# A transformer block on one core: the order of its first step, and where 128 side pieces are worked off

## The chip, the cores and the metric

The kernel runs on one core of a Trainium2 chip. The metric is the device time of one execution in microseconds (us), less is better. The kernel before takes 1694.38 us, the median of three runs between 1694.19 and 1694.40 us. The engines are named as in the profile: PE does the matrix products, DVE the work on vectors, ACT activations and copies, POOL small odd jobs and some transfers, SP issues most transfers.

## The reference

One layer works on 256 latent tokens and 256 context tokens of 2048 channels. Cut to what matters here:

```
h   = rms_norm(x) * g1 * (1 + scale) + shift          # shift, scale from silu(cond) @ w_ada + b_ada
p   = h @ w_in                                        # keys and values of all tokens, queries and gates of the latent ones
a   = grouped-query attention;  b = differential attention    # 2-D rotary, one softmax over latent and context keys
m   = sigmoid(g_a) * (a @ w_br_a) + sigmoid(g_b) * (b @ w_br_b)
x2  = x + gate * (m @ w_out)                          # gate: another chunk of w_ada
out = x2 + gate2 * swiglu_ffn(modulated rms_norm(x2)) # shift, scale, gate2: the last chunks of w_ada
```

Context tokens have a shift and a scale of their own. All of it is in 32-bit floats. The conditioning product `silu(cond) @ w_ada` has six chunks of 2048 columns.

## The kernel before, in words

**Products in three parts.** Every large product is made of three matmuls (`mm3`, L241 to L243): the weight is divided into a high part `whi` and a remainder `wlo`, the activation likewise. A weight tile of 128 x 1024 comes by a transfer of 512 KB into `wraw` (7 buffers, shared with the conditioning pieces `wada`), ACT casts it to `whi` (L235, 3 buffers) and DVE subtracts to get `wlo` (L237, 3 buffers). One such load feeds 24 matmuls of 512 columns. The second matmul of each three, L242, is the one that needs `wlo`.

**The start.** Conditioning vectors come in a small tile `head`, are turned on PE into `hps` (L108) and copied to `cst` and `vt` (L109, L111). The chunks shift and scale of the first norm are made on PE from pieces of `w_ada` (L315, tile `ada`), copied out by ACT (`asb`), turned on PE (`atp`, L325), summed by DVE (L328), and the bias is added (L331), then 1 + scale times g1 (L335). The function `ada_cond` does this in the steps of `STEPS`: one k-tile of 128 channels, one more, then 2, 4, 4 and 4. Meanwhile the second half of the tokens (the latent ones, tiles 2 and 3) and the context tokens (0 and 1) are squared, normed and, for the first k-tile, turned on PE (`xtp`, L378); ACT and DVE make the modulated high and low parts (L391 to L393). `keep_busy` issues idle 128 x 128 transposes on PE (L371). `kv_first` makes the key and value products of the first k-tile (L402).

**Channel steps.** Steps 1 to 5 go over the remaining channels. In each, `kv_group` runs the six column groups of keys and values, for four token tiles at once, and adds the sums from the PSUM tiles `mm` into the tiles kb, ka, vb, va (L443, DVE). In steps 3 to 5 a column group has two weight loads. During the last two groups of a step, DVE makes the modulated tiles of the next one (`hx` L357, `xT` and `cT` L361, eight of each).

**The pieces.** Four more chunks of `w_ada` are computed on DVE: `ada_later` is a generator of 128 pieces (L460 and L458), each with a transfer of 512 KB and one DVE instruction on 128 x 1024 elements. `take(later, n)` lets n pieces go at a place in the program. When a chunk is complete, `ada_row` sums it over partitions with four matmuls (`adac`), adds a row that POOL loads (`adac_sb`, and `adac_g` for one chunk, both from a pool `scr` of 3 buffers), and writes it to DRAM.

**After the steps.** Attention follows with the query and gate projections in between. A gate tile takes a buffer of the same pool `scr` when ACT evacuates it (L859), and POOL sends it to DRAM (`gate_d`, L860). Then come the merge (the product with `w_bra`, then `w_out`), and the feed-forward part.

**What sets the order.** A framework orders each engine's instructions before the run, from the program's order, its own estimates and `issue_after`. On the chip every engine takes its instructions strictly in that order, and waits for semaphores at the head. SP's and POOL's transfers are queues of the same kind.

Of the kernel before, what the change touches and what calls it, by code (L numbers as in the profile page):

```python
# [46 lines left out]
def hybrid_block(ctx: ExitStack, tc: tile.TileContext, t: dict, out: bass.AP):  # L47
# [35 lines left out]

    cst = scratch("cst", CG, tag="sq", bufs=2).rearrange("p (k m) -> p k m", m=32)
# [7 lines left out]
    ssq, r_tok = sums[:, 0:16].rearrange("p (i q) -> p i q", i=4), sums[:, 20:24]  # L92
    nc.gpsimd.memset(sums, EPS)
# [4 lines left out]
    def load_tokens(src, i):  # L98

        tok_in[i] = big_tile(f"tok{i}")  # L100
        for h in range(2):
            nc.sync.dma_start(out=tok_in[i][:, h * 2 * CG:(h + 1) * 2 * CG],
                              in_=src[0, i % 2 * P:(i % 2 + 1) * P, h * 2 * CG:(h + 1) * 2 * CG])
# [4 lines left out]
    nc.tensor.transpose(out=hps[:, 0:81], in_=head, identity=ident[0:81, 0:81])  # L108
# [6 lines left out]
    gsub = vt[:, 80:81]  # L115

# [10 lines left out]
    def squares_act(i, c0=CG, c1=3 * CG, late=None, to=0):  # L127
        mid = tok_in[i][:, c0:c1]
        with tc.issue_after(late.ins) if late else nullcontext():
            nc.scalar.activation(out=mid, in_=mid, func=AF.Square, scale=D ** -0.5, accum_out=ssq[:, i, to:to + 1])  # L130

    def squares_dve(i, parts=(0, 3), late=None):
        with tc.issue_after(late.ins) if late else nullcontext():
            for n, q in enumerate(parts):
# [3 lines left out]
                                                      accum_out=ssq[:, i, 1 + n:2 + n])  # L138
# [88 lines left out]
    def split_w(raw, nk, in_big=False, late=None):  # L227
# [6 lines left out]
        with tc.issue_after(late[0].ins) if late else nullcontext():  # L234
            last_hi.append(nc.scalar.copy(out=hi[:, 0:nk], in_=raw[:, 0:nk]))  # L235
        with tc.issue_after(late[1].ins) if late else nullcontext():
# [43 lines left out]
    def ada_cond(k0, nk):  # L280
# [4 lines left out]
        for part in range(2):  # L285
            aps = s_ps("ada")
            held = []
            for q in range(0, NKT, kk):
# [22 lines left out]
                first_ks, last_ks = (range(0, 4), range(12, 16)) if k0 == 0 else (range(4, 8), range(8, 12)) if k0 == 4 else (range(12, 16), range(0, 4))  # L311
                for k, rhs in held[::-1] if k0 else held:
# [4 lines left out]
                held = []  # L317
                if last:
# [3 lines left out]
                if last:  # L322
                    atp = tp_ps("atp")
                    for j in range(nk):
                        nc.tensor.transpose(out=atp[:, j * P:(j + 1) * P], in_=asb[:, j * P:(j + 1) * P], identity=ident)  # L325
                    m = small(f"mod{part}", 8)
                    mv = m[:, 0:2 * nk].rearrange("p (j w) -> p j w", w=2)
                    nc.vector.tensor_reduce(  # L328
                        out=mv, in_=atp[:, 0:ncol].rearrange("p (j g m) -> p j m g", g=4, m=32)[:, :, 0:2, :],
# [290 lines left out]
    def next_tokens(tok):  # L620
# [7 lines left out]
        if tok == 3:  # L628
            hold(0, (first_hi[-1], last_first[-1]))
# [553 lines left out]
```

## Time and profile before

| | |
|---|---|
| median of three runs | 1694.38 us |
| the profiled execution | 1696.49 us |
| its span | 1694.7 us |
| PE busy | 1675.7 us, 99% of the span |
| DVE busy | 1143.0 us, 67% |
| ACT busy | 776.4 us, 46% |
| transfers | 413.08 MB, mean 244 GB/s |
| an `ada` piece on DVE (L460) | 120 times, mean 1278 ns |
| a `wlo` subtraction on DVE (L237) | 498 times, mean 1220 ns |

About 1.8 us of the profiled execution lie outside its span. A row of the timeline gives the start in us from the span's beginning, the duration, the engine, line, operation, the tile written and those read, and in brackets the idle time before it with what ended it. Durations overlap: the next matmul of 512 columns starts 0.227 us after the one before, though the row says 0.39 us; the next `ada` piece or `wlo` on DVE starts 1.19 or 1.14 us later, a copy of 128 x 512 (L443) 0.60 us and a 128 x 256 instruction (L357, L361) 0.40 us later.

### The profile page before, as it was taken

What the parts mean: (1) busy time and instruction counts of PE and PEld (TensorE: products, weight loads), DVE (VectorE), ACT (ScalarE), POOL (GpSimd) and SP (SyncE); (2) the same over time, 40 slices, a digit from 0 to 9 for tenths busy, and PEclk for the clock granted to TensorE, in tenths of its full rate; (3) what the DMA queues carried; (4) which work ended last, traced back from release to release, by engine and by line L of the source; (5) the groups of instructions that cost most, each with busy time, mean ns of one, the idle gap of its engine ahead of it and who ended that gap; (6) DMA issues with size and microseconds to landing.
All of it is one profiled execution on the core that took longest, in us unless ns stands there. A gap on an engine that the chain in (4) does not pass through costs nothing.

```text
span 1694.7 us, 21499 instructions
## 1 busy us (share of the span) xinstructions
PE 1675.7 (99%) x7889; PEld 1354.8 (80%) x7889; DVE 1143.0 (67%) x1454; ACT 776.4 (46%) x1055; POOL 202.3 (12%) x296
## 2 busy tenths in 40 slices
PE   7999999999999999999999999999999999999998
PEld 5677778887887778888888888888888888888887
DVE  5765779697798888986666755566666666544454
ACT  5231222246666566667544534444444444333332
POOL 0200002011131110011111101111111111100000
PEclk9999999999999999999999999999999999999999
DMA  9888875777767767766877857888888898866662
GB/s 349 300 311 286 299 256 169 237 249 257 231 198 228 247 208 256 265 228 201 266 257 248 293 171 215 250 258 263 266 265 268 263 277 253 240 216 197 214 208 88
DMA packets 181284, 413.08 MB, mean 244 GB/s; under 512 B 15001, under 2 KB 16234, under 8 KB 180922
## 3 DMA queue, kind: packets, MB, share of 16 engines
q1 hardware_dynamic: 168906, 374.17, 67.3%
q0 software_dynamic: 12272, 37.53, 7.4%
q8 instruction: 62, 1.02, 0.3%
q14 instruction: 44, 0.36, 0.1%
HBM read 395.35 MB, written 16.29 MB: 243 GB/s over the span
## 4 chain that ended last, share of the span: by engine, by line
PE 92%; DVE 3%; DMA 2%; ACT 1%; issue 1%; POOL 0%; SPq 0%; DVEq 0%; ACTq 0%; POOLq 0%
PE mm L242 28%; PE mm L241 28%; PE mm L243 28%; PE ada L315 2%; PE ptp L815 1%; DVE wlo L237 1%; PE s L791 1%; PE mm L402 1%; PE o L836 1%; DMA wada<-in_ada_t_dram 1%; DMA wraw<-in_w_ff_gate_dram 0%; ACT whi L235 0%; DMA gate_d<-gate 0%; DMA wraw<-in_w_in_dram 0%; DVE ada L460 0%
## 5 line engine op out<-in xcount | busy, mean ns | idle before, releaser
L237 DVE TENSOR_TENSOR wlo<-wraw,whi 128x1024 fp32r<-128x1024 f32 x498 | 607.0, 1220 | 425.1 <-ACT whi L235 423.8
L235 ACT CAST whi<-wraw 128x1024 fp32r<-128x1024 f32 x498 | 522.8, 1051 | 727.1 <-PE mm L243 624.0
L242 PE MATMUL mm<-wlo,hT 128*128 128x512 f32 x684 | 266.2, 389 | 0.4 <-DVE wlo L237 0.4
L243 PE MATMUL mm<-whi,hT 128*128 128x512 f32 x684 | 266.1, 389 | 0.0
L241 PE MATMUL mm<-whi,hT 128*128 128x512 f32 x684 | 266.1, 389 | 0.0
L241 PE MATMUL mm<-whi,xT 128*128 128x512 f32 x630 | 251.9, 402 | 0.0
L242 PE MATMUL mm<-wlo,xT 128*128 128x512 f32 x630 | 247.3, 393 | 2.7 <-DVE wlo L237 2.7
L243 PE MATMUL mm<-whi,xT 128*128 128x512 f32 x630 | 246.8, 392 | 0.0
L460 DVE SCALAR_TENSOR_TENSOR ada<-wada,vt,ada 128x1024 f32<-128x1024 f32 x120 | 152.1, 1278 | 0.0
L242 PEld LDWEIGHTS mm<-wlo,hT 128*128 128x128 f32 x684 | 128.4, 188 | 27.7 <-DVE wlo L237 0.9
L241 PEld LDWEIGHTS mm<-whi,hT 128*128 128x128 f32 x684 | 128.4, 188 | 26.8
L243 PEld LDWEIGHTS mm<-whi,hT 128*128 128x128 f32 x684 | 128.4, 188 | 26.4
L241 PEld LDWEIGHTS mm<-whi,xT 128*128 128x128 f32 x630 | 118.2, 188 | 33.0 <-issue 6.6
L242 PEld LDWEIGHTS mm<-wlo,xT 128*128 128x128 f32 x630 | 118.8, 189 | 27.6 <-DVE wlo L237 5.0
L243 PEld LDWEIGHTS mm<-whi,xT 128*128 128x128 f32 x630 | 118.5, 188 | 25.8 <-DVE xT L361 0.3
L241 PE MATMUL mm<-whi,fT 128*128 128x512 f32 x354 | 137.5, 388 | 0.5 <-DVE y L1128 0.5
L242 PE MATMUL mm<-wlo,fT 128*128 128x512 f32 x354 | 137.3, 388 | 0.0
L243 PE MATMUL mm<-whi,fT 128*128 128x512 f32 x354 | 137.3, 388 | 0.0
L241 PEld LDWEIGHTS mm<-whi,fT 128*128 128x128 f32 x354 | 66.4, 188 | 15.0 <-issue 0.8
L243 PEld LDWEIGHTS mm<-whi,fT 128*128 128x128 f32 x354 | 66.4, 188 | 13.8
L242 PEld LDWEIGHTS mm<-wlo,fT 128*128 128x128 f32 x354 | 66.4, 188 | 13.7
L241 PE MATMUL mm<-whi,oT 128*128 128x512 f32 x192 | 75.9, 396 | 0.0
(236 smaller groups left out, 2142.7 us busy)
## 6 DMA issues: line engine op xcount, KB each, us to landing
wraw<-in_w_in_dram SPq DMA_DIRECT2D x159, 512.0 KB, 4.9
wada<-in_w_ada_dram SPq DMA_DIRECT2D x128, 512.0 KB, 4.7
wraw<-in_w_ff_gate_dram SPq DMA_DIRECT2D x88, 512.0 KB, 4.6
wraw<-in_w_ff_up_dram SPq DMA_DIRECT2D x88, 512.0 KB, 5.2
wraw<-in_w_ff_down_dram SPq DMA_DIRECT2D x88, 512.0 KB, 4.7
wada<-in_ada_t_dram SPq DMA_DIRECT2D x56, 512.0 KB, 6.6
wraw<-in_w_br_a_dram SPq DMA_DIRECT2D x32, 512.0 KB, 5.0
wraw<-in_w_out_dram SPq DMA_DIRECT2D x32, 512.0 KB, 5.1
```

The source lines that it names most:

```text
L235: last_hi.append(nc.scalar.copy(out=hi[:, 0:nk], in_=raw[:, 0:nk]))
L237: last_lo.append(nc.vector.tensor_tensor(out=lo[:, 0:nk], in0=raw[:, 0:nk], in1=hi[:, 0:nk].bitcast(F32), op=ALU.subtract))
L241: nc.tensor.matmul(ps, lhsT=ah, rhs=wh, start=first, stop=False, skip_group_check=skip)
L242: nc.tensor.matmul(ps, lhsT=ah, rhs=wl, start=False, stop=False, skip_group_check=skip)
L243: return nc.tensor.matmul(ps, lhsT=al, rhs=wh, start=False, stop=last, skip_group_check=skip)
L315: last_pe[0] = nc.tensor.matmul(aps[32 * g:32 * g + 32, 0:ncol], lhsT=cst[:, k, :], rhs=rhs, start=k in first_ks, stop=k in last_ks)
L402: last_pe[0] = nc.tensor.matmul(ps[cg], lhsT=x, rhs=ws0[cg][y], start=(n == 0), stop=(n == 2))
L460: nc.vector.scalar_tensor_tensor(out=dst, in0=wt, scalar=sc[:, 0, kt:kt + 1], in1=dst, op0=ALU.mult, op1=ALU.add)
L791: nc.tensor.matmul(sps[i], lhsT=qT[rows, x, hh, tk * P:(tk + 1) * P], rhs=kT["b", grp][y][rows, hh, :], start=(n == 0), stop=(n == 2))
L815: nc.tensor.transpose(out=tp[:, kt * P:(kt + 1) * P], in_=p[:, kt * P:(kt + 1) * P], identity=ident)
L836: nc.tensor.matmul(op[:, 0:BV], lhsT=pT[:, kt, :], rhs=vb[:, kt, hh * BV:(hh + 1) * BV], start=(kt == 0), stop=(kt == 3))
```

## The change

It has these parts.

- **Start.** Five idle transposes go to PE ahead of `hps`, thirty after it, three after the conditioning pieces of step 0 but the last, and ten before the second token tile (before: six, six and four). For step 0 the transpose of `asb` and the sum on DVE become one product with a selection matrix `sel` (two columns). 1 + scale times g1 is folded into the bias once (`vt_done`), so that L335 goes; wider steps have a multiplication with g1 more.
- **Second latent tile.** Token tile 3 is loaded as a half and two quarters, ahead of the second weight load; its squares are shared by ACT and DVE in quarters. The first weight cast is done in two halves. The products of tile 2 with the second weight stand behind the norm of tile 3.
- **Order of held pieces.** In steps 0, 2 and 3 of `STEPS` (k0 of 0, 2 and 4) the conditioning matmuls go over the held pieces forward instead of backward.
- **Pacing of the side pieces.** In step 3 one per half group, two in the last two groups (before: none, then two); in step 4 one, and two from the third group on (before: one throughout); in step 5 one per group (before: two). Later one at every third turn throughout (before: every second until the keys are done). The rest go in the `w_bra` products and in `w_out`, whose third column group now holds the `drain` and the loading of the row `b_all`, which stood before `w_out`.

```diff
-    nc.tensor.transpose(out=hps[:, 0:81], in_=head, identity=ident[0:81, 0:81])
+    idle = mm_ps("idle")
+    for _ in range(5):
+        nc.tensor.transpose(out=idle[:, 0:P], in_=ident, identity=ident)
+    last_pe = [None]
+    last_pe[0] = nc.tensor.transpose(out=hps[:, 0:81], in_=head, identity=ident[0:81, 0:81])
...
-                first_ks, last_ks = (range(0, 4), range(12, 16)) if k0 == 0 else (range(4, 8), range(8, 12)) if k0 == 4 else (range(12, 16), range(0, 4))
-                for k, rhs in held[::-1] if k0 else held:
+                first_ks, last_ks = (range(0, 4), range(12, 16)) if k0 in (0, 2, 4) else (range(12, 16), range(0, 4))
+                for k, rhs in held if k0 in (0, 2, 4) else held[::-1]:
...
+                if k0 == 0 and not (part and last):
+                    keep_busy(3)
...
+                    if k0 == 0:
+                        nc.tensor.matmul(atp[:, 0:2], lhsT=asb[:, 0:P], rhs=sel, start=True, stop=True)
...
-        nc.vector.scalar_tensor_tensor(out=scale, in0=scale, scalar=1.0,
-                                       in1=g1[:, k0:k0 + nk].unsqueeze(2).to_broadcast([P, nk, 2]), op0=ALU.add, op1=ALU.mult)
...
+    keep_busy(30)
     squares_act(2)
-    squares_dve(2)
+    squares_dve(2, late=vt_done)
...
-    keep_busy(6)
-    drain(ada_cond(*steps[0]))
+    ada_0 = ada_cond(*steps[0])
+    take(ada_0, 2)
+    with tc.issue_after(last_pe[0].ins):
+        turn_first(2)
+    drain(ada_0)
...
-    raws = {cg: load_raw(0, cg * CG) for cg in (2, 4)}
-    load_tokens(t["x"], 3)
+    raws = {2: load_raw(0, 2 * CG)}
+    load_tokens(t["x"], 3, (0, 2, 3, 4))
+    raws[4] = load_raw(0, 4 * CG)
...
     next_tokens(3)
+    hold(4, (last_copy[0], last_first[-1]))
+    kv_first(2, (4, 5), (0, 1))
     kv_first(3, (2, 3))
+    kv_first(2, (4, 5), (2,))
     kv_first(3, (4, 5))
...
-                if si == 3 and n >= 4:
-                    take(later, 2)
-                elif si > 3:
+                if si in (3, 4):
+                    take(later, 2 if n >= (4 if si == 3 else 2) else 1)
+                elif si == 5 and half == 0:
                     take(later, 1)
...
-            take(later, 1 if turns[0] % (3 if a_done else 2) else 0)
+            take(later, 1 if turns[0] % 3 == 0 else 0)
...
-    drain(later)
-    b_all = ada_everywhere("b_all", 2)
...
     for cg in range(4):
-        drain(project(w_out, mT, NKT, cg * CG, out_evac(cg), **(dict(tail=TURN2, hook=tail_hook, in_big=(6, 7)) if cg == 3 else {})))
+        if cg == 2:
+            drain(later)
+            b_all = ada_everywhere("b_all", 2)
+        for k, _ in enumerate(project(w_out, mT, NKT, cg * CG, out_evac(cg), **(dict(tail=TURN2, hook=tail_hook, in_big=(6, 7)) if cg == 3 else {}))):
+            if k in (2, 5, 6) and (cg or k > 4):
+                take(later, 1)
```

**First place: step 4 begins.** DVE, before. The weight of the first group of step 4 is `wraw_1648`; its products go to the PSUM tiles `mm_1644` to `mm_1647`. The tiles `mm_1504` to `mm_1507` belong to the last group of step 3.

```order
L331 TENSOR_TENSOR mod1_1484<-mod1_1484,vt_99 128x8
L237 TENSOR_TENSOR wlo_1651<-wraw_1648,whi_1650 128x1024
L335 SCALAR_TENSOR_TENSOR mod1_1484<-mod1_1484,vt_99 128x8
L206 TENSOR_REDUCE lam_1603<-used_691 128x2
L357 SCALAR_TENSOR_TENSOR hx_1489<-tok_t2_1040,mod1_1484,r_all_447 128x256 x2
L357 SCALAR_TENSOR_TENSOR hx_1497<-tok_t2_1040,mod1_1484,r_all_447 128x256 x2
L357 SCALAR_TENSOR_TENSOR hx_1584<-tok_t2_1040,mod1_1484,r_all_447 128x256 x2
L361 SCALAR_TENSOR_TENSOR xT2_1490<-hx_1489,mod0_1256,xT2_1490 128x256 x2
L361 SCALAR_TENSOR_TENSOR xT2_1490<-hx_1497,mod0_1256,xT2_1490 128x256 x2
L443 TENSOR_TENSOR va0_102<-mm_1504,va0_102 128x512
L361 SCALAR_TENSOR_TENSOR cT_1488<-hx_1584,mod0_1256,cT_1488 128x256
L443 TENSOR_TENSOR va0_102<-mm_1505,va0_102 128x512
```

The same of the change (L237 is now L247, L443 is L472, L357 and L361 are L379 and L383). The weight of that group is `wraw_1723`, the last group of step 3 is in `mm_1579` to `mm_1582`.

```order
L383 SCALAR_TENSOR_TENSOR xT2_1565<-hx_1572,mod0_1314,xT2_1565 128x256
L383 SCALAR_TENSOR_TENSOR cT_1563<-hx_1659,mod0_1314,cT_1563 128x256
L472 TENSOR_TENSOR va0_112<-mm_1580,va0_112 128x512
L379 SCALAR_TENSOR_TENSOR hx_1659<-tok_t2_1091,mod1_1554,r_all_499 128x256
L379 SCALAR_TENSOR_TENSOR hx_1666<-tok_t2_1091,mod1_1554,r_all_499 128x256
L472 TENSOR_TENSOR va0_112<-mm_1581,va0_112 128x512
L383 SCALAR_TENSOR_TENSOR cT_1563<-hx_1659,mod0_1314,cT_1563 128x256
L472 TENSOR_TENSOR va0_112<-mm_1582,va0_112 128x512
L383 SCALAR_TENSOR_TENSOR cT_1563<-hx_1666,mod0_1314,cT_1563 128x256
L379 SCALAR_TENSOR_TENSOR hx_1666<-tok_t2_1091,mod1_1554,r_all_499 128x256
L214 TENSOR_REDUCE lam_1678<-used_742 128x2
L247 TENSOR_TENSOR wlo_1726<-wraw_1723,whi_1725 128x1024
```

The first `wlo` of step 4 stood ahead of the modulated tiles and of all four va sums; it now stands behind the fourth. PE at the same place, of the change:

```order
L253 MATMUL mm_1582<-whi_1621,cT_1023 128x512
L251 MATMUL mm_1719<-whi_1725,xT2_1565 128x512
L251 MATMUL mm_1720<-whi_1725,xT2_1565 128x512
L251 MATMUL mm_1721<-whi_1725,cT_1563 128x512
L251 MATMUL mm_1722<-whi_1725,cT_1563 128x512
L252 MATMUL mm_1719<-wlo_1726,xT2_1565 128x512
```

Four matmuls of the high part now stand ahead of the first with `wlo`; before there was one.

**Second place: step 5 begins.** DVE, before; the weight is `wraw_2215`, and `mm_2123` is the first sum of the last group of step 4.

```order
L328 TENSOR_REDUCE mod1_2103<-atp_2098 128x8
L331 TENSOR_TENSOR mod1_2103<-mod1_2103,vt_99 128x8
L237 TENSOR_TENSOR wlo_2218<-wraw_2215,whi_2217 128x1024
L335 SCALAR_TENSOR_TENSOR mod1_2103<-mod1_2103,vt_99 128x8
L460 SCALAR_TENSOR_TENSOR ada2_1433<-wada2_2195,vt_99,ada2_1433 128x1024
L357 SCALAR_TENSOR_TENSOR hx_2108<-tok_t3_1598,mod1_2103,r_all_447 128x256 x2
```

The change; the weight is `wraw_2324`, and `mm_2218` to `mm_2221` are the last group of step 4.

```order
L472 TENSOR_TENSOR va0_112<-mm_2218,va0_112 128x512
L472 TENSOR_TENSOR va0_112<-mm_2219,va0_112 128x512
L379 SCALAR_TENSOR_TENSOR hx_2306<-tok_t3_1673,mod1_2193,r_all_499 128x256
L472 TENSOR_TENSOR va0_112<-mm_2220,va0_112 128x512
L383 SCALAR_TENSOR_TENSOR cT_2202<-hx_2306,mod0_1939,cT_2202 128x256
L472 TENSOR_TENSOR va0_112<-mm_2221,va0_112 128x512
L379 SCALAR_TENSOR_TENSOR hx_2306<-tok_t3_1673,mod1_2193,r_all_499 128x256
L379 SCALAR_TENSOR_TENSOR hx_2313<-tok_t3_1673,mod1_2193,r_all_499 128x256 x2
L383 SCALAR_TENSOR_TENSOR cT_2202<-hx_2306,mod0_1939,cT_2202 128x256
L383 SCALAR_TENSOR_TENSOR cT_2202<-hx_2313,mod0_1939,cT_2202 128x256 x2
L247 TENSOR_TENSOR wlo_2327<-wraw_2324,whi_2326 128x1024
```

Again the first `wlo` of the step has moved from ahead of the modulated tiles to behind the fourth va sum, here with six small instructions between.

**Third place: the gates in attention.** POOL, before: a pair of gate tiles, with the two row loads for a chunk's sum around its second.

```order
L860 DMA gate_d_2733<-gate_4772 128x512
L467 DMA adac_sb_5188<-in_rows_dram 128x512
L860 DMA gate_d_2733<-gate_4775 128x512
L467 DMA adac_g_5267<-in_rows_dram 128x512
L124 TENSOR_TENSOR rstdo_4815<-rstdo_4815,neghalf_80 128x1
```

The change:

```order
L895 DMA gate_d_2822<-gate_4829 128x512
L496 DMA adac_sb_5372<-in_rows_dram 128x512
L895 DMA gate_d_2822<-gate_4832 128x512
L132 TENSOR_TENSOR rstdo_4872<-rstdo_4872,neghalf_80 128x1
```

The load of `adac_g` is no longer there; it now follows the next pair of gate tiles.

More of the change, by code (lines that the diff above doesn't have):

```diff
@@ L82, in hybrid_block @@
     nc.gpsimd.memset(ones, 1.0)
+    sel = tab.tile([P, 2], F32, name="sel")
+    nc.vector.tensor_reduce(out=sel, in_=ident.rearrange("p (g m) -> p m g", m=32)[:, 0:2, :], axis=AX.X, op=ALU.add)
     cst = scratch("cst", CG, tag="sq", bufs=2).rearrange("p (k m) -> p k m", m=32)
@@ L322, in ada_cond @@
                 if last:
-                    atp = tp_ps("atp")
-                    for j in range(nk):
-                        nc.tensor.transpose(out=atp[:, j * P:(j + 1) * P], in_=asb[:, j * P:(j + 1) * P], identity=ident)
                     m = small(f"mod{part}", 8)
                     mv = m[:, 0:2 * nk].rearrange("p (j w) -> p j w", w=2)
-                    nc.vector.tensor_reduce(
-                        out=mv, in_=atp[:, 0:ncol].rearrange("p (j g m) -> p j m g", g=4, m=32)[:, :, 0:2, :],
-                        axis=AX.X, op=ALU.add)
@@ L331, in ada_cond @@
[L331 to L332 removed]
+                    atp = tp_ps("atp")
+                    base = bada[:, part * NKT + k0:part * NKT + k0 + nk].unsqueeze(2).to_broadcast([P, nk, 2])
+                    gain = g1[:, k0:k0 + nk].unsqueeze(2).to_broadcast([P, nk, 2])
+                    if k0 == 0:
+                        nc.tensor.matmul(atp[:, 0:2], lhsT=asb[:, 0:P], rhs=sel, start=True, stop=True)
+                        ms = atp[:, 0:2].rearrange("p (j w) -> p j w", w=2)
+                    else:
+                        for j in range(nk):
+                            nc.tensor.transpose(out=atp[:, j * P:(j + 1) * P], in_=asb[:, j * P:(j + 1) * P], identity=ident)
+                        nc.vector.tensor_reduce(
+                            out=mv, in_=atp[:, 0:ncol].rearrange("p (j g m) -> p j m g", g=4, m=32)[:, :, 0:2, :],
+                            axis=AX.X, op=ALU.add)
+                        ms = mv
@@ L627, in next_tokens @@
         mod_first(tok)
-        if tok == 3:
-            hold(0, (first_hi[-1], last_first[-1]))
     next_tokens(3)
+    hold(4, (last_copy[0], last_first[-1]))
+    kv_first(2, (4, 5), (0, 1))
     kv_first(3, (2, 3))
+    kv_first(2, (4, 5), (2,))
     kv_first(3, (4, 5))
+    hold(0, (first_hi[-1], last_lo[-1]))
+    ada_1 = ada_cond(*steps[1])
     kv_first(2, (0,))
     next_tokens(0)
-    kv_first(3, (0,), True)
+    kv_first(3, (0,), behind=True)
     kv_first(0, (2, 3))
@@ L640, in hybrid_block @@
     next_tokens(1)
-    kv_first(0, (0,), True)
+    kv_first(0, (0,), behind=True)
     kv_first(1, (2, 3))
```

63 lines of the change are left out of this document (37 added, 26 removed).

## The prediction

> **What bounds the kernel now.** I read the page first, then the list of what PE waited for, whole and by stretches, then PE and DVE row by row where the change works.
>
> ```profile
> PE 1675.7 (99%) x7889; PEld 1354.8 (80%) x7889; DVE 1143.0 (67%) x1454; ACT 776.4 (46%) x1055; POOL 202.3 (12%) x296
> PE 92%; DVE 3%; DMA 2%; ACT 1%; issue 1%; POOL 0%; SPq 0%; DVEq 0%; ACTq 0%; POOLq 0%
> ```
>
> PE is busy for 1675.7 of 1694.7 us, and 92% of the chain that ended last is PE's. The change leaves the large products alone. So it can save only out of the 19 us in which PE stands still, and whatever new wait it gives PE is paid in full. Where are those 19 us? PE's waits over the span (us in total, times, longest):
>
> ```profile
> PE ada L315 <- DMA wada<-in_ada_t_dram: 6.0, 2, 5.3
> PE mm L242 <- DVE wlo L237: 3.1, 4, 1.9
> ```
>
> Busy time by stretches says which stage is loose:
>
> ```profile
> 0.00:17.00 17.00, 7.89 (x81) 5.37 (x81) 3.32 (x14) 4.85 (x10) 2.03 (x12) 1.00 0.88 312
> 17.00:40.00 23.00, 22.03 (x148) 16.03 (x149) 16.26 (x35) 16.69 (x31) 1.66 (x3) 1.00 1.01 389
> 100.00:310.00 210.00, 210.00 (x1003) 164.47 (x1002) 157.26 (x231) 55.34 (x74) 10.59 (x5) 1.00 0.74 259
> ```
>
> After the times come PE, PEld, DVE, ACT and POOL busy, the granted clock (1.00 throughout), the share of the transfers and GB/s. Half the idle time lies in the first 17 us. In the channel steps from 100 to 310 us PE has none at all, while DVE is busy for 157 of 210 us: a stage where an addition to DVE finds no PE time to win, and can only lose some.
>
> **The change part by part.**
>
> Start. PE and the short chain to the first key product:
>
> ```profile
> 2.91 0.37 PE L108 MATMUL hps<-ident,head 81*128 81x81 f32 x1 [2.91 <-ACT head L106]
> 8.54 1.82 PE L315 MATMUL ada<-wada,cst 128*32 128x128 f32 x18 [5.26 <-DMA wada<-in_ada_t_dram]
> 10.77 1.49 PE L371 MATMUL idle<-ident 128*128 128x128 f32 x6
> 12.19 1.51 PE L315 MATMUL ada<-wada,cst 128*32 128x128 f32 x24
> 14.04 1.19 PE L315 MATMUL ada<-wada,cst 128*32 128x128 f32 x22
> 15.29 0.27 ACT L320 COPY asb<-ada 128x128 f32<-128x128 f32 x1 [1.71 <-PE ada L315]
> 15.98 0.17 DVE L328 TENSOR_REDUCE mod<-atp 128x2 f32<-128x8 f32 x1 [1.47 <-PE atp L325]
> 16.18 0.16 DVE L331 TENSOR_TENSOR mod<-mod,vt 128x2 f32<-128x2 f32 x1
> 16.38 0.16 DVE L335 SCALAR_TENSOR_TENSOR mod<-mod,vt 128x2 f32<-128x2 f32 x1
> 17.09 1.19 PE L402 MATMUL mm<-whi,xT 128*128 128x512 f32 x4 [0.92 <-ACT xT L391]
> ```
>
> The conditioning matmuls cost 1.82/18 = 0.10 us at first and 1.19/22 = 0.054 us from 14.04 on: PE runs at half pace until about 4 us after it has become nearly continuously busy, though the granted clock reads 1.00. If the idle transposes bring that on early, a piece of 16 matmuls costs 0.9 instead of 1.6 us. Of the 64 matmuls 42 ran slowly, so 42 x 0.046 = 1.9 us go, and two of the three small DVE steps, 0.4 us: 2.3 us earlier at 17.09. The added transposes stand in the 5.26 us between `hps` and the first piece, so at fast pace they cost nothing; uncovered, thirty cost 30 x 0.11 = 3.3 us. What is late next is the first context tile:
>
> ```profile
> 24.19 0.16 DVE L143 TENSOR_REDUCE sums<-sums 128x1 f32<-128x4 f32 x1 [0.18 <-ACT tok L130]
> 25.01 0.29 DVE L146 TENSOR_SCALAR tok<-tok,sums 128x128 f32<-128x128 f32 x1 [0.66 <-POOL sums L144]
> 25.75 0.38 PE L378 MATMUL xtp<-ident,tok 128*128 128x128 f32 x2
> ```
>
> Its norm comes through DVE, which in the new order first does two subtractions of 1.14 us and two quarters of squares. PE's products of the latent tiles finish 2 us earlier, this chain does not follow all the way. The bounds are 0 and 2.3 us; I take **-0.8**, nearer the lower, since what stands ahead on DVE is about as much as before.
>
> [...]
>
> Forward order of the held pieces. One wait goes:
>
> ```profile
> 62.45 1.06 PE L315 MATMUL ada<-wada,cst 128*32 128x512 f32 x8 [0.72 <-DMA wada<-in_ada_t_dram]
> ```
>
> Backward, the eight begin with the piece that landed last; forward, six that are there go first, 6 x 1.06/8 = 0.8 us, which covers it: **-0.8**, between 0 and that.
>
> Channel steps. Pieces in step 3 go from 8 to 16, in step 4 from 12 to 20, in step 5 from 12 to 6. DVE has room on the average. Its order is what costs. Where step 4 begins, before:
>
> ```profile
> 169.94 1.22 DVE L237 TENSOR_TENSOR wlo<-wraw,whi 128x1024 fp32r<-128x1024 f32 x1
> 179.08 0.39 PE L241 MATMUL mm<-whi,xT 128*128 128x512 f32 x1
> 179.31 0.39 PE L242 MATMUL mm<-wlo,xT 128*128 128x512 f32 x1
> 179.42 0.68 DVE L443 TENSOR_TENSOR va<-mm,va 128x512 f32<-128x512 f32 x1
> ```
>
> This `wlo` was ready at 171.16, 8 us ahead. With the added pieces it now stands behind the fourth va sum, which waits for PE to end the group, at 179.42. Behind that sum (0.60) come two 128 x 256 instructions (0.40 each), one `lam` sum (0.19), then `wlo` itself (1.22): ready at 182.23. PE has four high-part matmuls ahead, so it wants it at 179.08 + 4 x 0.227 = 179.99: **+2.2**. All further products and the DVE work of the group queue behind.
>
> In the middle of step 4 the `wlo` of the third group's second load moves from ahead of a modulation sum to behind it:
>
> ```profile
> 210.08 0.60 PE L325 MATMUL atp<-ident,asb 128*128 128x128 f32 x4
> 210.43 0.47 PE L241 MATMUL mm<-whi,xT 128*128 128x512 f32 x1
> 212.91 0.18 DVE L328 TENSOR_REDUCE mod<-atp 128x8 f32<-128x32 f32 x1
> 213.12 0.17 DVE L331 TENSOR_TENSOR mod<-mod,vt 128x8 f32<-128x8 f32 x1
> ```
>
> The sum cannot start before the transposes end at 210.68. With 0.07 for the signal, 0.21 and 0.09 for the two rows and 1.22 for `wlo` it is ready at 212.27; PE wants it at 210.43 + 0.91 = 211.34: **+0.9**.
>
> Where step 5 begins, the same as at step 4:
>
> ```profile
> 242.82 1.23 DVE L237 TENSOR_TENSOR wlo<-wraw,whi 128x1024 fp32r<-128x1024 f32 x1
> 252.65 0.39 PE L243 MATMUL mm<-whi,cT 128*128 128x512 f32 x1
> 252.88 0.39 PE L241 MATMUL mm<-whi,xT 128*128 128x512 f32 x1
> 254.10 0.68 DVE L443 TENSOR_TENSOR va<-mm,va 128x512 f32<-128x512 f32 x1
> ```
>
> The group ends at 253.04, the fourth va sum starts at about 253.15 and takes 0.60; three hx and three cT follow (6 x 0.40), then `wlo` 1.22: ready at 257.37. Wanted at 252.88 + 0.91 = 253.79: **+3.6**. Two more places are within 0.2 us of waiting; with them the channel steps give **+6.9**. The lower bound is 0, if the engine's order let these through; I see no way past a semaphore at the head of DVE, and take the sum. The upper is 8.5, if also the transfers, now 3 x 512 KB per load in part, land late.
>
> Attention. Two waits for `wlo` between 300 and 800 us, then POOL and PE at their cause, then one piece of the chain of waits:
>
> ```profile
> PE mm L242 <- DVE wlo L237: 2.4, 2, 1.9
> ```
>
> ```profile
> 531.28 0.55 POOL L467 DMA_DIRECT2D adac_sb<-in_rows_dram  x1
> 536.53 0.55 POOL L467 DMA_DIRECT2D adac_g<-in_rows_dram  x1 [4.17 <-issue]
> 628.05 0.50 PE L242 MATMUL mm<-wlo,xT 128*128 128x512 f32 x1 [1.86 <-DVE wlo L237]
> ```
>
> ```profile
> 586.77 6.75 DMA gate_d<-gate
> ```
>
> From 531 on the two rows hold two of three buffers, so the next pair of gates must share one: the chain shows 6.75 us for the transfer of the first, ACT's casts get late, DVE bunches, and at 628.05 PE waits. In the change `adac_g` comes after that pair, and fewer pieces stand on DVE: -2.4. Against it a piece and two subtractions now stand ahead of one `wlo`:
>
> ```profile
> 370.86 1.22 DVE L237 TENSOR_TENSOR wlo<-wraw,whi 128x1024 fp32r<-128x1024 f32 x1
> 372.91 0.40 PE L242 MATMUL mm<-wlo,xT 128*128 128x512 f32 x1
> ```
>
> Added are 1.19 + 2 x 0.33 = 1.85 us against 372.91 - 372.08 = 0.83 us to spare: +1.0. Together **-1.4**, between -2.4 and +1.0.
>
> Merge. Sixteen more pieces, 19 us of DVE and 16 transfers, in a stretch of 170 us where DVE was busy 110: hidden by PE on the average, up to 1 us where they stand ahead of a `wlo`: **+0.3**.
>
> Sum: -0.8 - 0.8 + 6.9 - 1.4 + 0.3 = **+4.2** without what overlaps; the 0.9 at 210 shrinks when PE is already 2 us behind and DVE has caught up, so I take **+3.8**. The profiled execution, 1694.7 us of span and 1.8 around it, would go from 1696.5 to 1700.3; the median stands 2.1 us lower, so **1698.2**.
>
> **The rivals.**
>
> *DVE's order costs nowhere.* Then the 6.9 go, and so do the 1.0 at 371 us and the 0.3 of the merge, which I priced in the same way: -0.8 - 0.8 - 2.4 = -4.0, or 1690.4. For it: DVE is only 75% busy in the channel steps. Against it: the fourth va sum needs PE's last matmul of the group. It decides if the first `wlo` of steps 4 and 5 ends within 0.9 us of the group's end.
>
> *The transposes warm nothing.* Thirty at 1.49/6 = 0.25 us end near 3.3 + 7.4 = 10.7, past the 8.54 of the first piece. Pieces then start 2 us late, reach the fast pace only some 4 us on, and the first product comes 0.8 us later than now instead of earlier: 1.6 us on top, 1699.8. [...]
>
> *The merge chokes.* The second half of each `w_bra` product has four pieces more, 4.8 us of DVE in 10.9. If each of the four runs past the spare there by 0.7 us, 2.8 on top: 1701.
>
> *The gains come whole.* The new waits stand, but the start gives its 2.3 (1.5 more) and attention its 2.4 (1.0 more): 1695.7, no change. For it: 1.5 us of the start are held back only by a chain on DVE that the new order rearranges.
>
> **How the numbers follow.** A measurement here tells 0.2%, 3.4 us, from no change: 1691.0 and 1697.8. My forecast, 1698.2, has 0.49, of which 0.21 lies below 1697.8. The first rival has 0.25, as faster; the second 0.11 and the third 0.07, slower; the fourth 0.08, same. Faster 0.25, same 0.29, slower 0.28 + 0.18 = 0.46. The forecast's own range is 1695.5 to 1700.5. The range over all reaches to the first rival and to the third: 1690.2 to 1701.
>
> **What would show it.** In the changed profile PE should wait for `wlo` some 2 us at about 179 and 3.5 us at about 252, and these two should be the longest in the list after the start. The conditioning matmuls at 8.5 us should cost 0.054 us each, the first key product should start near 15 and the first context product near 25.9. The waits at 62 and 628 should be gone. No wait for `wlo` between 150 and 300 us makes the prediction wrong, whatever the time.

## The result, and the profile after

The change makes the kernel slower: 1706.61 us (median of 6 runs, 1704.26 to 1708.59) against 1694.39 us (6 runs, 1693.48 to 1695.41). The ratio is 1.0070, with a 95% interval of 1.0057 to 1.0083. That is 12 us more where 3.8 were forecast, and outside the range. The profiled execution took 1707.28 us, 10.8 us more than that of before.

The page of the changed kernel:

```profile
span 1705.5 us, 21596 instructions
PE 1686.3 (99%) x7935; PEld 1361.3 (80%) x7935; DVE 1145.5 (67%) x1454; ACT 777.8 (46%) x1056; POOL 194.2 (11%) x297
```

PE stands still for 19.2 us, as before (19.0), yet it is busy for 10.6 us more. With both traces cut at the same matmuls, 4.5 us of this lie in the first 37 us, where idle transposes were added, 2.3 in the stretch up to 103 us and 7.5 in the channel steps up to 317 us; attention is 5.1 us less busy. What it waited for, over the span:

```profile
PE mm L252 <- DVE wlo L247: 5.1, 4, 3.0
PE mm L251 <- ACT whi L245: 2.1, 2, 1.1
PE o L871 <- DVE qT L257: 1.2, 1, 1.2
PE ada L325 <- DMA wada<-in_ada_t_dram: 0.8, 1, 0.8
```

The wait for the first conditioning piece has shrunk from 5.3 us to 0.8. In its place stand waits for weights in the channel steps; the stretch from 100 to 310 us shows them (after the times PE, PEld, DVE, ACT and POOL busy, granted clock, share of the transfers, GB/s):

```profile
100.00:310.00 210.00, 202.03 (x943) 153.73 (x942) 158.17 (x230) 52.74 (x71) 9.07 (x6) 0.98 0.76 273
```

From 100 to 310 us PE was busy all the time before; now it lacks 8 us there, and has done 943 of 1003 instructions. DVE's time over the whole stretch is the same (158.17 against 157.26), so it is its order and the places of its work that have changed. The granted clock is 0.98 there, where it was 1.00.

Where the time went can be read by laying the two traces side by side: the start of the same matmul with `wlo` in both (worked out from the two traces: after less before, at the times of before):

```
before, us   37.8  102.7 176.6 192.9 213.5 233.6 250.4 266.7 301.5 555.6 578.6 620.5 646.6 812.6 1687.5
difference  -0.97  +0.34 +0.54 +5.12 +7.06 +9.46 +10.2 +15.5 +15.8 +14.8 +12.8 +15.2 +11.4 +9.57 +10.29
```

Four stairs of the channel steps make it, and attention gives some back. A chunk's row sum on PE (`adac`), 1.2 us, has moved between stretches; it is taken out where sums are named below. One correction to the description ahead: of the 128 pieces 96 come from `ada_later`; the other 32 are those of the feed-forward's modulation.

PE where step 4 begins, after the change:

```profile
179.62 0.61 PE L251 MATMUL mm<-whi,xT 128*128 128x512 f32 x2
181.27 0.49 PE L251 MATMUL mm<-whi,cT 128*128 128x512 f32 x1 [0.43 <-DVE va L472]
183.38 0.75 PE L252 MATMUL mm<-wlo,xT 128*128 128x512 f32 x1 [1.62 <-DVE wlo L247]
183.93 0.63 PE L253 MATMUL mm<-whi,xT 128*128 128x512 f32 x1
184.36 0.63 PE L251 MATMUL mm<-whi,xT 128*128 128x512 f32 x1
186.49 0.57 PE L251 MATMUL mm<-whi,xT 128*128 128x512 f32 x1
186.90 0.40 PE L252 MATMUL mm<-wlo,xT 128*128 128x512 f32 x1
```

DVE ahead of it, and its busy time in the stretch that leads there:

```profile
180.53 0.68 DVE L472 TENSOR_TENSOR va<-mm,va 128x512 f32<-128x512 f32 x1
182.12 1.21 DVE L247 TENSOR_TENSOR wlo<-wraw,whi 128x1024 fp32r<-128x1024 f32 x1
158.00:183.20 25.20, 25.20 (x42) 1.00 1.00 381
```

As forecast, `wlo` stands behind the fourth va sum. DVE had no idle moment in the 25 us ahead of it. PE wanted it at 179.62 + 4 x 0.227 = 180.53 and had it at 183.38: 2.85 us. Then comes what was not forecast: the next matmuls start 0.43 us apart (183.93, 184.36, and so on to 186.49), against 0.227 otherwise, and only from 186.90 on at the usual distance. These slow matmuls cost another 1.7 us. The same at step 5:

```profile
263.10 0.62 PE L251 MATMUL mm<-whi,xT 128*128 128x512 f32 x2
...
267.55 0.50 PE L252 MATMUL mm<-wlo,xT 128*128 128x512 f32 x1 [3.00 <-DVE wlo L247]
268.79 0.61 PE L252 MATMUL mm<-wlo,xT 128*128 128x512 f32 x1
271.76 0.60 PE L251 MATMUL mm<-whi,cT 128*128 128x512 f32 x1
272.19 0.41 PE L252 MATMUL mm<-wlo,cT 128*128 128x512 f32 x1
```

Here the four high-part matmuls began at 263.10, `wlo` was wanted at 264.01 and came at 267.55: 3.54 us, and eight slow matmuls cost about 1.6 more, 8 x (0.43 - 0.227). In stretches of 4 us (PE busy, granted clock, share of the transfers, GB/s):

```profile
184.00:188.00 4.00, 4.00 (x13) 0.64 0.83 225
212.00:216.00 4.00, 3.80 (x19) 1.00 1.03 410
216.00:220.00 4.00, 3.05 (x12) 1.00 1.03 405
236.00:240.00 4.00, 3.03 (x14) 1.00 1.01 383
268.00:272.00 4.00, 4.00 (x13) 0.60 0.81 250
```

After the two long waits the granted clock is 0.64 and 0.60. At 212 to 220 and at 236 us it is 1.00 but the transfers are full (1.01 to 1.03): there `whi` was late because its raw weight was (ACT's casts at 215.78 and 238.30 each waited for the transfer of `wraw`). The stretches 212 to 224 and 236 to 244 us of the kernel before had shares of 0.64 and 0.77:

```profile
212.00:224.00 12.00, 12.00 (x67) 1.00 0.64 237
236.00:244.00 8.00, 8.00 (x39) 1.00 0.77 251
```

### The profile page after: what moved, and what is told of

Its sections match the earlier page's. It is cut to its first block, busy times and chain, and to the rows that moved or that the text cites. A ratio compares the mean times of both kernels' runs of the same rounds, so it can differ in the third digit from the quotient of the medians.

```text
span 1705.5 us, 21596 instructions
## 1 busy us (share of the span) xinstructions
PE 1686.3 (99%) x7935; PEld 1361.3 (80%) x7935; DVE 1145.5 (67%) x1454; ACT 777.8 (46%) x1056; POOL 194.2 (11%) x297
## 3 DMA queue, kind: packets, MB, share of 16 engines
q8 instruction: 62, 1.02, 0.2%
## 4 chain that ended last, share of the span: by engine, by line
PE 91%; DVE 4%; DMA 3%; issue 1%; ACT 1%; POOL 0%; SPq 0%; DVEq 0%; ACTq 0%; POOLq 0%
PE mm L252 27%; PE mm L253 27%; PE mm L251 27%; PE ada L325 1%; DMA wraw<-in_w_in_dram 1%; PE ptp L850 1%; DVE wlo L247 1%; PE o L871 1%; PE mm L429 1%; PE s L826 1%; ACT whi L245 0%; DMA wada<-in_w_ada_dram 0%; PE s L251 0%; DVE ada L489 0%; PE o L251 0%
## 5 line engine op out<-in xcount | busy, mean ns | idle before, releaser
L247 DVE TENSOR_TENSOR wlo<-wraw,whi 128x1024 fp32r<-128x1024 f32 x498 | 606.7, 1219 | 440.3 <-ACT whi L245 439.0
L245 ACT CAST whi<-wraw 128x1024 fp32r<-128x1024 f32 (+1 forms) x499 | 523.4, 1049 | 749.1 <-PE mm L253 589.6
```

The source lines that it names most:

```text
L245: last_hi.append(nc.scalar.copy(out=hi[:, n * by:(n + 1) * by], in_=raw[:, n * by:(n + 1) * by]))
L247: last_lo.append(nc.vector.tensor_tensor(out=lo[:, 0:nk], in0=raw[:, 0:nk], in1=hi[:, 0:nk].bitcast(F32), op=ALU.subtract))
```

## The experiments

**My theory after the result:** the new numbers of pieces in steps 3 to 5 alone make the loss, through DVE's order at the two step starts, through PE's slow matmuls after a long wait, and through late transfers at 215 and 238 us. **Its rivals:** the start and the new order of the held pieces carry part of it; the later places of the pieces (attention, merge) do.

**The new numbers of pieces alone, in the kernel before.**

```diff
-                if si == 3 and n >= 4:
-                    take(later, 2)
-                elif si > 3:
+                if si in (3, 4):
+                    take(later, 2 if n >= (4 if si == 3 else 2) else 1)
+                elif si == 5 and half == 0:
                     take(later, 1)
```

> The kernel before with nothing but the new numbers of side pieces in channel steps 3 to 5. Theory A (the pacing of the pieces makes the loss in the channel steps: in the changed profile the products fall 15.2 us behind between 160 and 300 us, about 0.9 of it a moved row sum): the same waits appear, at about 180 us and 262 us, and the time is 1694.4 + 14 less up to 4 us that attention gives back, 1703 to 1708. Theory B (the new start, the forward order or the merge make it): within 2 us of before, at most 1697.

Measured: 1708.53 us, ratio 1.0082 (1.0067 to 1.0097). Its waits between 150 and 310 us:

```profile
PE mm L242 <- DVE wlo L237: 4.8, 3, 3.0
```

That is the changed kernel's own row for the same stretch (4.8, 3 times, longest 3.0), with slow matmuls again behind the waits, from 184.48 to 187.04 and from 266.29 to 269.28 us, and a granted clock of 0.98 between 100 and 310 us. This one edit makes the whole loss, and the time lies a little above the 1703 to 1708 us expected. All the other parts together give back some 2 us; as the two intervals overlap, even that is not sure.

**The old numbers in the changed kernel.** The same edit the other way.

> The changed kernel with the numbers of side pieces in channel steps 3 to 5 of before. Theory A: no wait of PE for a weight part between 150 and 300 us, 1706.6 - 14 = 1692, up to 1695 if attention and merge get crowded by the pieces that are left. Theory B: 1702 or more.

Measured: 1702.23 us, ratio 1.0046 (1.0031 to 1.0061). PE has no wait at all from 150 to 310 us, and 15.4 us less than the changed kernel by the end of the steps, as expected. But the end shows 4.4 us, since behind 812 us 10.1 of them come back, nearly all in `w_out`. PE there, and the stretch around it:

```profile
923.35 1.22 PE L251 MATMUL mm<-whi,mT 128*128 128x512 f32 x2 [5.65 <-ACT whi L245]
```

```profile
920.00:930.00 10.00, 6.55 (x16) 2.73 (x17) 9.12 (x11) 4.37 (x7) 3.28 (x6) 0.66 1.02 330
```

The number of pieces is fixed. With fewer in the steps, and with the change's slower pace in attention, 11 are left for the `drain` ahead of the third column group of `w_out` (in the change 1). Their transfers stand ahead of the weight on SP's queue (share 1.02), PE waits 5.65 us, and the clock drops to 0.66 after it. Pieces taken from one stage return in the tightest place behind it. The time lies where the rival expected it (1702 or more), but not for the rival's reason: the waits of the channel steps went as my theory said, and I had left out what the other pieces do later.

**Step 4 alone back to one piece per half group.**

```diff
-                if si in (3, 4):
-                    take(later, 2 if n >= (4 if si == 3 else 2) else 1)
-                elif si == 5 and half == 0:
+                if si == 3:
+                    take(later, 2 if n >= 4 else 1)
+                elif si == 4 or (si == 5 and half == 0):
```

> The changed kernel with one piece per half group throughout step 4, as before; step 3 and step 5 keep the new numbers. Theory A, with each step's pieces answering for the start of the next step: the wait at 181 us stays (about 4.6 us with what follows it), those at 215, 238 and 264 us go (1.9 + 2.4 + 5.3): 1706.6 - 9.6 = 1697. If instead the total of pieces per step mattered and not the order at the step's start: the wait at 181 goes too, 1692.

Measured: 1708.84 us, ratio 1.0086 (1.0071 to 1.0101), where about 1697 was expected. By the same reading of matmul starts, the wait at 181 stayed and those at 215, 238 and 264 went (1.2, 2.4 and 5.3 us): 9 us less at 300 us, as the theory had it. All of it was given back later: with the moved row sums taken out, 1.0 us at 709, 1.2 between 838 and 863, and 6.8 in `w_out`, by the left-over pieces again. The places were right, the end was wrong, since I had not asked where eight pieces would go.

**The first weight of steps 4 and 5 one load earlier in the program.** The pace stays that of the change; its first load in these steps is merely prepared before the group's last products.

```diff
+    ahead = {}
...
-                    wt[j // WK] = load_w(w_in, (k0 + j) * P, cg * CG, WK)
+                    wt[j // WK] = ahead.pop((k0 + j, cg), None) or load_w(w_in, (k0 + j) * P, cg * CG, WK)
+                    if nxt0 and j >= WK:        # nxt0: first group of the next step; steps 3 and 4, last group
+                        ahead[nxt0] = load_w(w_in, nxt0[0] * P, nxt0[1] * CG, WK)
```

> The changed kernel with all its pieces, but the first weight load of steps 4 and 5 stands one load earlier in the program, ahead of the last sums of the step before. Theory A (order on DVE: the weight part stands behind a sum that waits for PE): the waits at 181 and 264 us go with the slow matmuls after them, those at 215 and 238 stay: 1706.6 - 9 = 1697 to 1699. Rival (DVE or the transfers are simply too full there, whatever the order): the wait comes back at the loads after, and the time falls by less than 3 us.

Measured: 1698.51 us (10 runs), ratio 1.0026 (1.0016 to 1.0035), inside what was expected. Waits from 150 to 310 us:

```profile
PE mm L251 <- ACT whi L245: 2.5, 2, 1.5
PE mm L252 <- DVE wlo L247: 0.9, 2, 0.7
```

The two long waits are gone, with them every slow matmul (3.6 us less at step 4, 5.0 at step 5). Nothing was given back, since the pieces stayed where they were. So it was the place of `wlo` behind the va sums on DVE, and not the number of pieces as such. The two waits for late `whi` remain: these are the transfers'.

**Idle transposes in the two long waits.** Sixteen (end of step 3) and 28 (end of step 4) go to PE behind the group's last product, into a free PSUM tile. The waits are not mended, only filled.

```diff
+            if fill and n + 1 == len(order):    # fill: 16 in step 3, 28 in step 4, last group
+                idle = s_ps("idle")
+                with tc.issue_after(last_mm.ins):
+                    for _ in range(fill):
+                        nc.tensor.transpose(out=idle[:, 0:P], in_=ident, identity=ident)
```

> The changed kernel with idle transposes on PE in the two long waits: 16 after the last product of step 3, 28 after that of step 4 (1.7 and 3.1 us). The waits for the weight part stay in length, only filled. Theory (a wait of over about 2 us makes PE fall to half pace for some 3 us afterwards, 1.6 us lost each time, in most but not all executions): no slow matmuls after 184 and 268 us, the granted clock is 1.00 in all runs, the time about 1704 with a narrow spread. Rival (the slow matmuls come from something else, such as the transfers, or idle transposes don't count): slow matmuls and spread as in the changed kernel, 1706 to 1707.

Measured: 1704.8 us, ratio 1.0059 (1.0042 to 1.0076); the changed kernel stood at 1.0070 (1.0057 to 1.0083). PE at step 4, and at a later, unfilled wait:

```profile
179.74 1.91 PE L471 MATMUL idle<-ident 128*128 128x128 f32 x16
183.61 0.50 PE L252 MATMUL mm<-wlo,xT 128*128 128x512 f32 x1 [1.04 <-DVE wlo L247]
183.95 0.39 PE L253 MATMUL mm<-whi,xT 128*128 128x512 f32 x1
...
216.09 0.73 PE L251 MATMUL mm<-whi,xT 128*128 128x512 f32 x2 [1.65 <-ACT whi L245]
```

With the wait filled, the matmul after it lasts 0.39 us instead of 0.63, and none at half pace follows at 184 or 268. That fits PE's standing still as the cause of the slow matmuls; as unfilled waits are not always followed by slow ones either (two runs below), this one trace does not show it for sure. In this run seven at half pace (217.86 to 220.42, about 0.63 us each) came after the unfilled wait of 1.65 us at 216, where the change itself had waited 1.08 and had none. They cost about 1.4 us, half of what the filling gained, and the two totals cannot be told apart.

**The start without its transposes.** Five and thirty become one and one.

```diff
-    for _ in range(5):
+    for _ in range(1):
...
-    keep_busy(30)
+    keep_busy(1)
```

> The changed kernel with one idle transpose instead of five ahead of the head's, and one instead of thirty after it. Theory (the transposes bring PE to its full pace): the conditioning matmuls start at half pace (0.10 us each instead of 0.04), the first key product starts 1 to 2 us later than 14.79. Rival (transposes warm nothing): pace and first product as in the changed kernel.

Measured: 1709.64 us, a single run. PE without them:

```profile
9.23 1.08 PE L325 MATMUL ada<-wada,cst 128*32 128x128 f32 x16 [5.73 <-DMA wada<-in_ada_t_dram]
16.54 1.47 PE L429 MATMUL mm<-whi,xT 128*128 128x512 f32 x4 [0.53 <-ACT xT L413]
```

and with them, in the changed kernel:

```profile
3.15 4.82 PE L393 MATMUL idle<-ident 128*128 128x128 f32 x30
8.77 0.65 PE L325 MATMUL ada<-wada,cst 128*32 128x128 f32 x16 [0.80 <-DMA wada<-in_ada_t_dram]
14.79 1.29 PE L429 MATMUL mm<-whi,xT 128*128 128x512 f32 x4 [0.60 <-ACT xT L413]
```

The transposes do what they are there for: sixteen conditioning matmuls take 0.65 us instead of 1.08, and the first product starts 1.75 us earlier.

**The held pieces backward again.** The old `first_ks, last_ks` line and `held[::-1] if k0 else held` in the changed kernel.

> The changed kernel with the held conditioning pieces taken backward again, as before. In the changed profile the lead over before shrinks from 0.97 us at 37 us to a lag of 0.34 at 103 us, and the conditioning matmuls stand in three more blocks. Theory (each block that is divided costs PE about 0.4 us of change-over, 1.2 in all, more than the 0.8 us wait that goes): three blocks fewer, and at 103 us the products are about 0.5 us earlier than in the changed kernel. As the prediction had it: 0.8 us later.

Measured: 1703.32 us, a single run. At 103 us it stood 1.13 us ahead of the kernel before, where the change stood 0.34 behind: the forward order costs 1.5 us, where a gain of 0.8 was forecast. The other traces agree: between 38 and 103 us the seven with the forward order took 1.30 to 1.36 us more than the kernel before, the five others 0.07 to 0.51 less. What it does on PE, in the changed kernel:

```profile
61.27 1.90 PE L325 MATMUL ada<-wada,cst 128*32 128x512 f32 x10
68.78 1.06 PE L325 MATMUL ada<-wada,cst 128*32 128x512 f32 x6
86.43 1.04 PE L325 MATMUL ada<-wada,cst 128*32 128x512 f32 x2
92.18 1.92 PE L325 MATMUL ada<-wada,cst 128*32 128x512 f32 x14
```

The same 32 matmuls with the backward order:

```profile
61.77 1.06 PE L325 MATMUL ada<-wada,cst 128*32 128x512 f32 x8 [0.50 <-DMA wada<-in_ada_t_dram]
68.47 1.07 PE L325 MATMUL ada<-wada,cst 128*32 128x512 f32 x8
90.70 1.92 PE L325 MATMUL ada<-wada,cst 128*32 128x512 f32 x16
```

The wait of 0.50 us has gone, as forecast. But these matmuls, which write four groups of 32 output rows in turn, run four at a time here: in the trace of the kernel before four start at 92.29 to 92.31 us, and the next four at 92.72. A block that is not a multiple of four leaves ones and threes, which took as long as a four: 14 last as long as 16 (1.92), 6 as long as 8, 10 last 0.84 us longer than 8, and the two at 86.43 push the next product back by 1.07. That is 0.84 + 1.07 - 0.50 = 1.4 of the 1.5 us. The first block, of 256 columns, is divided in both runs. Why the blocks were cut at these places the profile does not show.

In this run the waits for `wlo` at the two step starts were there too, as long as in the change:

```profile
181.90 0.50 PE L252 MATMUL mm<-wlo,xT 128*128 128x512 f32 x1 [1.61 <-DVE wlo L247]
264.47 0.50 PE L252 MATMUL mm<-wlo,xT 128*128 128x512 f32 x1 [3.00 <-DVE wlo L247]
264.80 0.40 PE L253 MATMUL mm<-whi,xT 128*128 128x512 f32 x1
264.00:268.00 4.00, 3.53 (x15) 1.00 0.56 171
```

Yet no matmul at half pace followed either of them, and the two stairs were 3.0 us lower together. So slow matmuls do not follow every such wait.

**The old numbers everywhere**, steps, attention and merge, with the change's start and forward order kept.

> The changed kernel with the pieces paced everywhere as before: channel steps as before, and one at every second turn until the keys are done. The run with the old channel pacing alone lost 10.8 us in w_out, where PE waited 5.6 us for a weight behind the left-over pieces. Theory (the new pacing serves only to empty the list before w_out, and everything else of the change is worth 1 us at the start and up to 5 in attention): no left-over pieces, no wait at 915 us, 1688 to 1692. Rival (attention's gain came from having fewer pieces there): the waits at 571 and 628 us are back and the time is 1693 to 1695.

Measured: 1697.15 us (10 runs), ratio 1.0013 (1.0004 to 1.0022). Waits between 310 and 800 us:

```profile
PE mm L252 <- DVE wlo L247: 2.4, 2, 1.8
```

These two waits are those of the kernel before, at 571 and 628 us (2.4, 2 times, longest 1.9). So the gain in attention did come with the pacing, as the rival had it, though the time lies above both ranges that were written down. What the start, the forward order and the moved loading of `b_all` leave is a loss of 0.13%, less than a measurement tells for sure.

**The gates' buffer, alone, in the kernel before.** `adac_g` takes a large tile of its own instead of one from the pool `scr`.

```diff
-    r = scratch(name)
+    r = big_tile(name)[:, 0:CG] if n == 4 else scratch(name)
```

> The kernel before, with the second row that a chunk's sum needs (adac_g) in a large buffer of its own instead of one of the three that the gates use. Theory (two rows in three buffers make the second gate wait for the first's transfer, casts and subtractions come late, PE waits at 628 us and then runs slowly: 3.1 us in the two profiles): no wait of ACT for the gate's transfer, no wait of PE at 628, 1691 to 1692. Rival (the pieces on DVE make that wait, as their number does in the changed kernel): the wait stays, 1694.

Measured: 1692.03 us (10 runs) against 1694.63 (21 runs), ratio 0.9985 (0.9976 to 0.9994). POOL at the pair of gates:

```profile
585.54 0.58 POOL L860 DMA_DIRECT2D gate_d<-gate  x1 [4.98 <-ACT gate L859]
586.90 0.54 POOL L860 DMA_DIRECT2D gate_d<-gate  x1 [0.78 <-ACT gate L859]
```

The second gate leaves at 586.90; before it left at 594.49. PE's wait of 1.86 us at 628 is gone, and by the matmul starts 3.9 us with it, because in the profiled execution of the kernel before slow matmuls had stood behind that wait too (0.63 us each, 0.43 apart, from here to 631.99); the first of them:

```profile
629.43 0.63 PE L241 MATMUL mm<-whi,xT 128*128 128x512 f32 x1
```

The medians differ by 2.6 us. In the run with the old numbers everywhere the same wait (1.84 us, at 630) had no slow matmuls behind it, so executions without them gain less than 3.9. This version beats both kernels, the one before by less than the 0.2% that a measurement tells for sure, though its interval excludes 1.

**The new start with it**: the change's first step, with the backward order, the old numbers, and the buffer.

> The changed kernel with all pieces paced as before, the held pieces backward as before, and the row in a buffer of its own: what is left is the start (warm-up, selection product, quarters) and the moved loading of b_all. Theory (the start is worth 1.1 us once the blocks are whole, the buffer 3): 1690 to 1691.5, faster than before. Rival (the start's lead is lost again on the way to the end): as the run before it in this list.

Measured: 1692.2 us (11 runs), ratio 0.9985 (0.9977 to 0.9994): the same as without the new start, as the rival had it. Over the traces with the new start and its transposes the first product starts at 14.4 to 15.5 us, against 16.4 to 17.1 with the old one, but the first matmul with `wlo` of the steps stands at 36.8 to 37.5 us, against 37.1 to 37.8.

**A third in attention, paid in `w_bra`.** Old numbers in the steps, backward order, the change's pace in attention, and the pieces that are then left in all but the first of a `w_bra` product's parts.

```diff
-            if k > 3:                                # w_bra; w_out stays as in the change
+            if k > 0:
                 take(later, 1)
```

> The changed kernel with the channel pacing of before, backward order, one piece at every third turn in attention as in the change, and the rest in the w_bra products from their second load on (7 in each), so that none is left for w_out. Theory (the change's pacing is good for attention, 3.9 us by the profiles, and harmful only in the channel steps): 1694 - 1.1 - 3.9 = 1689, up to 1692 if the w_bra products get crowded. Rival (DVE and the transfers are too full in w_bra): new waits between 810 and 880 us and 1694 or more.

Measured: 1700.31 us (5 runs), ratio 1.0038 (1.0024 to 1.0052). The `w_bra` stretch of this run, and of the change:

```profile
795.00:890.00 95.00, 90.24 (x397) 71.76 (x396) 82.78 (x85) 43.01 (x54) 11.46 (x21) 0.98 0.98 353
```

```profile
795.00:890.00 95.00, 95.00 (x441) 78.51 (x440) 78.55 (x84) 50.79 (x66) 13.88 (x26) 1.00 0.93 322
```

Up to 812 us the kernel is 4.4 us ahead of the one before, the moved row sum taken out: attention's gain is there. Between 822 and 899 us it loses 9.0, as the rival had it. The change holds this stretch at a share of transfers of 0.93 without a wait; at 0.98 PE lacks 4.8 us, and the granted clock falls to 0.98.

## Why the prediction was wrong, step by step

**What bounds the kernel** was read rightly: PE is the bound, new waits are paid in full, and the channel steps are the place. The sign was right, and slower was the likeliest of the three outcomes.

**Channel steps: the term that was mis-sized.** "+6.9", and with late transfers "8.5" as the upper bound, measured 14.1 (15.3 between 176.6 and 301.5 us, less the moved row sum of 1.2):

| place | forecast | measured |
|---|---|---|
| start of step 4, wait | 2.2 | 2.9 |
| slow matmuls behind it | not seen | 1.7 |
| middle of step 4 (215 us) | 0.9 | 1.9 |
| 238 us, `whi` late | within the 0.2 | 2.4 |
| start of step 5, wait | 3.6 | 3.54 |
| slow matmuls behind it | not seen | 1.6 |

The order at both step starts was read rightly, `wlo` behind the fourth va sum, and at step 5 the wait came to within 0.06 us. At step 4 the fourth va sum ran 0.6 us later than assumed. The forecast let it wait for PE; in fact DVE, busy without a break since 158 us, still had the third sum and one `cT` instruction ahead of it. Two things were missing, and they are the step that failed: the sum put the time behind a wait at nothing, and the late transfers too low. The waits of 1.62 and 3.00 us in the change were followed by 3.4 us of PE at half pace each (granted clock 0.50 from 183.46 to 186.88 and from 268.80 to 272.21 us); the rows behind the wait at 628 us of the kernel before already showed it, unread, and those at 8.5 to 14 us showed the pace itself. And the late transfers were named as a bound and priced at 1.6 us at most. At 215 and 238 us they ended the waits, 1.9 and 2.4 us; the modulation sum, from which the 0.9 was forecast, was done at 216.23, and `wlo` then waited for `whi` until 216.86. Beyond the 0.9 that makes 3.4.

**Attention: the term that was too small.** "-1.4" measured -3.9 (6.25 between 301.5 and 812.6 us, less two moved row sums). The wait at 628 took its slow matmuls with it: 3.9 by itself between these two traces, as the buffer alone showed, where its 1.9 us were counted. The "+1.0" at 371 was a wait of 0.26 us, at 388 us of the change; a new wait of 1.2 us (`o`, L871) stands against the rest.

**Order of the held pieces: the wrong sign.** "-0.8" was 1.5 the other way. "Six that are there go first, which covers it" held, for the wait went. The step that failed is the price of the matmuls themselves: the new blocks broke up groups of four that run together, which was put at nothing.

**Start.** "-0.8" was about -0.3 over the traces, a difference no larger than that between runs. The first product near 15 (14.79) held, the conditioning matmuls were faster than the 0.054 us forecast (0.65 / 16 = 0.041), and the reason for taking little held too: the context tile's norm on DVE does not follow.

**Merge.** "+0.3" was -0.5 (0.72 between 812.6 and 1687.5 us, less the moved row sum of 1.2), with no wait in `w_bra`.

**The rivals.** That DVE's order costs nowhere is refuted by the result, by the new numbers alone and by the earlier first load. That the transposes warm nothing is refuted by the run without them. That the merge chokes did not happen here, but the last run shows it, a few pieces on. That the gains come whole was half right: attention gave more than its 2.4, the start not its 2.3.

**What stays open.** The six runs of the change are spread: two took 1704.3 us at a granted clock of 1.000, one 1706.1 at 0.999, three 1707 to 1709 at 0.997 to 0.998. The 3 us are about the price of the slow matmuls (1.7 + 1.6), and the run with the backward order shows the same two waits without them, 3.0 us cheaper at the two stairs. So most likely they do not occur in the quicker executions; of the change itself only one with them was profiled, so for it this is argued and not shown.

## What to carry to other kernels

Before moving side work, look on the engine it runs on for what then waits at the head of its queue: the last evacuation of a group ahead of the first weight of the next costs the bound engine the whole chain between them, though DVE was busy for only 75% of the stage as a whole; issuing that one weight a load earlier won 8 of 12 us. Price a wait of PE with what can follow it: here slow matmuls added 1.7 us to one of 2.9 and 1.6 to one of 3.54, and nothing to waits as long in another run. Do not break up groups of small matmuls that run together: here it cost 1.4 of the 1.5 us that the forward order lost, the wait it saved counted in. Follow moved pieces to where they end up, since a fixed number of them comes back at the tightest place behind. The cheapest gain here was no order at all but one more buffer where two uses shared a pool.

## What the runs showed of the hardware

- Matmuls at half pace followed some short waits of PE and not others. After 1.62 us of waiting (on top of 0.43) and after 3.00 us in the change, 7 to 8 matmuls of 512 columns started 0.43 us apart instead of 0.227, at a granted clock of 0.64 and 0.60 over 4 us; after 1.86 us in the kernel before (at 628 us) and after 1.65 us in the filled run (at 216 us) it was seven. In the last run, whose longest waits between 800 and 890 us were of 0.9 and 0.8 us, the granted clock was 0.98 from 795 to 890 us. After 1.61 and 3.00 us in the run with the backward order, 1.84 us in the one with the old numbers everywhere (granted clock 1.000 over the whole run) and 1.5 us in the one with the earlier load (1.00 from 100 to 310 us) there were none.
- In the trace of the kernel before, the granted clock was 0.50 from 629.17 to 632.59 us; in that of the change from 183.46 to 186.88 and from 268.80 to 272.21 us: 3.41 us each time. The two drops of the change begin 85.34 us apart, 25 times this length. With both traces cut into stretches of this length from the drops on, and without the first 20 us and the end, PE stood still for 1.86 us of the stretch ahead of the one drop and for 2.18 and 2.17 us ahead of the other two, and for at most 1.15 us of any other (238.07 to 241.49 us of the change), with the clock at 1.00 behind it. This is worked out from these two traces only; why the run with the backward order had none after waits of the same length is not shown.
- The drop did not come at once each time: after the wait of 3.00 us in the change the first matmuls still started about 0.23 us apart, and those at half pace began 1.2 us later, at 268.79.
- With sixteen idle transposes of 128 x 128 floats in the wait at step 4 of the filled run, the second matmul behind it took 0.39 us (at 183.95), where in the change it took 0.63 (at 183.93). With thirty-five at the start of the change, sixteen conditioning matmuls took 0.65 us from 8.77 us on; with two they took 1.08 at 9.23 and at 11.08 us, and 0.65 first at 13.27. The 1.00 that the first rows of the kernel before give as the granted clock stands where its trace has no clock record: these begin at 14.78 us (in the change at 5.97), and up to 14.69 us four conditioning matmuls of 128 columns started every 0.21 us, from 14.84 on every 0.11.
- Conditioning matmuls of 32 output rows and 512 columns ran four at a time in 0.43 us; one or three took as long as four (86.43 and 93.06 us of the change). Between 36 and 104 us there are 128 conditioning matmuls, half of them of 256 columns; they take 38 such turns in the change and 32 in the kernel before.
